# First sweep of an fp32 GLA and conv-FFN layer: row statistics squared in place and summed on VectorE, and one row split at a higher rank

## The chip, the cores and the metric

The kernel runs on one core of a Trainium2 chip. A core has a TensorE (PE; its weight loads are shown apart, as PEld), a VectorE (DVE), a ScalarE (ACT), a GpSimd (POOL) and a SyncE (SP), each working through its own list of instructions in order, and sixteen DMA engines, which take transfers from queues that SP, ACT and POOL issue to. The metric is the device time of one execution in microseconds (us); a run's number is the median of several.

## The reference

One layer over x, 2048 rows of 1024 float32 values. In the first half of the layer the rows are normalized, mixed by a gated linear attention and added back; the second half is a feed-forward network with a causal convolution over the rows:

```python
def rms_normalize(x):
    return x * lax.rsqrt(jnp.mean(x * x, axis=-1, keepdims=True) + EPS)   # EPS = 1e-6
h = rms_normalize(x) * w
proj = h @ w_in                       # columns: q 512, k 512, v 1024, r 1024, gate 16
log_a = log_sigmoid(glr @ w_gate2 + b_gate) / 16
g = cumsum(log_a) in chunks of 64 rows;  k_dec = k * exp(g_end - g)
state = state * exp(g_end) + k_dec^T v;  o = q state        # chunk by chunk, 4 heads
x = x + (rms_normalize(o) * norm_w * silu(r)) @ w_out
...                                   # then the FFN: 1024 -> 5632, convolution, silu(g) * val, 2816 -> 1024
```

## The kernel before

**Products.** Every matrix product of fp32 numbers is made of three products of halves. `split` rounds a block to a short high half on ScalarE (the CAST, L194) and subtracts that from the block on VectorE to get the low half (L195); `mm3p` then multiplies high by low, low by high and high by high (L185, L186, L187). On top of this stands a scheme with seven products in place of eight for a 2 by 2 block of tiles: `PORD` lists them as p1, p5, p6, p2, p7, p3, p4. They need sums and differences of the blocks as operands, which VectorE makes. The 2048 rows are sixteen tiles of 128 rows, and two tiles make a unit, so there are eight units.

**Stages.** The whole is a row of sweeps over the eight units: R (the r columns, and beside them the 16 gate columns), A and B (q, k, v and the scan), Y (w_out), and then the two phases of the FFN. The change touches the first sweep, R. There the rows come in transposed (`xt`, 512 KB a tile) and are multiplied by the norm weight (`hb_t_k`, tile t, half k; L462). The factor 1/rms of a row, `rs[:, t]`, is not in that product: it is put in when a result leaves PE's accumulators, by the evictions on ScalarE (`o_R` L1077 in the first unit, `cp_R` L1220 and `o_R` L1236 later) and on VectorE. So no eviction of tile t can run before `rs` of tile t is known.

**The statistics.** `squares()` makes them from a second load of x, not transposed: `load_rows` (L423, issued by ScalarE) brings half a tile of rows, 128 by 512, into `xr_t_i`, which has two buffers; a Square on ScalarE (L435) sums the squares of each row into `ssq_a`; then ScalarE issues the load of the half after the next one, into the buffer that the Square has just read. The squares themselves are not wanted and go to a tile `junk`, which takes one of the four buffers of the tag "cp"; the evictions `cp_R` use the same four. After a tile's second half GpSimd adds the two sums (L440), scales by 1/1024 and adds EPS (L441) and raises to the power of -0.5 (L442). `squares()` is called nine times by hand in the first unit, and after that four times per unit through a list of delayed calls.

**The first unit.** `first_pair` handles unit 0 with eight plain products m00 to m11 while it makes the operands that unit 1 needs: the weights w_R_p5, w_R_p2, w_R_p6, w_R_p7 (`sum5`, `sum6`, `sum7` in VectorE; each is also split), the differences `ht_1_o` of the rows of unit 1, and the split rows `h_R1_o` (`prep_rows`). The first of these, h_R1_p1, is split from hb_2_0 as it stands.

**The gate.** For each unit the 16 gate columns collect in `pg`, are split into `gstk` (L600 to L602), and for every four tiles a block runs: two matmuls, a softplus, a split into `lh` and `ll`, a cumulative sum on PE (`pd`), its exponential on ScalarE (`e`, L641), four transposes of that on PE (`pe`, L632) and a copy of the totals (`dec`, L634). `e_0_3` below is that exponential for tile 3.

**Order.** A list scheduler of the framework sets each engine's order: among the instructions whose inputs and buffers it expects to be free, it takes the one of the highest priority, which is by default the place in the program; `tc.high_priority(n)` moves it ahead by n. The code's own clock (`later_do`, by modelled PE time) decides at which place a delayed call stands. A tile of a tag with few buffers waits for the last reader of the tile that had the buffer.

Of the kernel before, what the change touches and what calls it, by code (L numbers as in the profile page):

```python
# [12 lines left out]
BF16 = mybir.dt.bfloat16  # L13
AF = mybir.ActivationFunctionType
ALU = mybir.AluOpType

P = 128
EPS = 1e-6
# [7 lines left out]
def hybrid_kernel(  # L26
# [17 lines left out]
    nc = tc.nc  # L44
# [5 lines left out]
    S, D = x.shape  # L50
# [41 lines left out]
    PORD = ("p1", "p5", "p6", "p2", "p7", "p3", "p4")  # L92
# [8 lines left out]
    gp = gx.enter_context(tc.tile_pool(name="gp", bufs=1))  # L101
# [36 lines left out]
    def raw_tile(shape, name):  # L138
        return wr.tile(shape, F32, tag="raw", name=name, bufs=RB)
# [79 lines left out]
    def small(tag, name, n=1):  # L219
        return cst.tile([P, 2], F32, tag=tag, name=name, bufs=4)[:, :n]  # L220
# [198 lines left out]
    def load_rows(m, q):  # L419
        t, i = divmod(m, 2)  # L420
        if t < NTT:
            xrow[m] = rp["h"].tile([P, 512], F32, tag="xr", name=f"xr_{t}_{i}", bufs=2)
            q.dma_start(xrow[m], x[t * P:(t + 1) * P, 512 * i:512 * (i + 1)])  # L423
# [3 lines left out]
    def squares():  # L427

        t, i = divmod(sq["n"], 2)
        r = xrow.pop(sq["n"])  # L430
        if i == 0:
            sq["ssq"] = small("ssq", f"ssq_a{t}", 2)
        ssq = sq["ssq"]
        junk = gp.tile([P, 1024], BF16, tag="cp", name=f"junk_{t}_{i}", bufs=4)
        nc.scalar.activation(junk[:, :512], r, AF.Square, accum_out=ssq[:, i:i + 1])  # L435
        load_rows(sq["n"] + 2, nc.scalar)
        sq["n"] += 1
        if i == 1:
            var = small("var", f"var_a{t}")
            nc.gpsimd.tensor_add(var, ssq[:, 0:1], ssq[:, 1:2])  # L440
            nc.gpsimd.tensor_scalar(var, var, 1.0 / D, EPS, op0=ALU.mult, op1=ALU.add)  # L441
            nc.gpsimd.tensor_tensor(rs[:, t:t + 1], var, neghalf, op=ALU.pow)  # L442

    def hb_tile(name):
# [41 lines left out]
    def prep_row(ps_, j, o):  # L486
        if ps_ == "R":
            need(f"h{j}")
            if o == "p4":
                b21, t2 = hsrc.pop(("p4", j))  # L490
                nc.vector.tensor_sub(b21, b21, t2)
                hsrc[j, o] = b21
            split_row(ps_, j, o, hsrc.pop((j, o)))
        else:
            m = jobs.index((ps_, j, o))
            for n in range(m, min(m + HB - 1, len(jobs))):
                if jobs[n] not in hraw:
                    p_, j_, o_ = jobs[n]
                    hraw[jobs[n]] = row_tile(f"hr_{p_}{j_}_{o_}")
                    nc.sync.dma_start(hraw[jobs[n]], (yd if p_ == "Y" else h1d)[j_, o_])  # L500
            split_row(ps_, j, o, hraw.pop((ps_, j, o)))
# [441 lines left out]
    def prep_rows(n):  # L943
        while done["rows"] < min(n, len(jobs)):
            prep_row(*jobs[done["rows"]])
            done["rows"] += 1
# [25 lines left out]
    def first_pair():  # L972
# [65 lines left out]
        def sum5():  # L1038
            for k in range(2):
                nc.vector.tensor_add(s_[V[k]], a21[V[k]], a22[V[k]])  # L1040
            split_sum("p5", [s_[V[k]] for k in range(2)])
# [49 lines left out]
        for k in range(2):  # L1091
            r = raw_tile([P, 2, 512], f"wr_{ps_}_{k}")
            load_block(put_act, r, ps_, k, (0, 1))
            a12.append(r)
        need_raw[0, 1] = a12
        squares()
        product(1, 0, 0)
        squares()
        product(1, 0, 1)
        squares()  # L1100
        weight("p2", (0, 1), "p2")
        squares()
# [5 lines left out]
        squares()  # L1108
        gate_plain(j, 1, 1, *h[1, 1])
        done["rows"] = len(PORD)  # L1110
        prep_rows(len(PORD) + 1)
        sum5()
        squares()
        product(0, 1, 0)
# [437 lines left out]
    nc.sync.dma_start(nwt, mix_norm_w)  # L1552
    xin[0] = load_xt(0, 2)
    first_pair()
    nc.scalar.dma_start(nw2, ffn_norm_w)
    nc.scalar.dma_start(gw, gla_norm_w)
# [136 lines left out]
```

## Time and profile before

| | |
|---|---|
| runs | 2101.47, 2102.18, 2104.19 us; median 2102.18 |
| the profiled execution | 2099.98 us, of which the traced span 2098.3 us |
| granted clock of TensorE over the span | 0.993 |
| TensorE busy | 98% of the span |
| VectorE, ScalarE, GpSimd busy | 75%, 53%, 33% |

A row of the timeline gives the start and the duration in us, the engine, the line, the operation, what it writes and reads, the shapes, and in brackets how long the engine had waited before it and for what. Names in these rows leave out the numbers of tile and product. Line numbers are those of the kernel before; in the changed one, lines after L441 are one lower up to the second edit.

### The profile page before, as it was taken

The numbers are of one execution on the slowest core, as the hardware profiler recorded it, in microseconds if no ns is written. First come the engines' busy times: TensorE is split into PE (matmuls) and PEld (weight loads), VectorE is DVE, ScalarE is ACT, GpSimd is POOL, SyncE is SP. The second block draws the span as 40 slices with busy tenths as digits, with TensorE's granted clock in tenths as the row PEclk, the third lists the DMA queues.
The fourth block names the chain that finished last, engine by engine and source line by source line (L and its number), as shares of the span: only waits on it lengthen the run. The fifth ranks groups of instructions, "written<-read, shape, count | busy, mean of one in ns | idle before, by whom it ended". The sixth has DMA issues, their size and how long they took to land.

```text
span 2098.3 us, 28206 instructions
## 1 busy us (share of the span) xinstructions
PE 2047.3 (98%) x9700; PEld 1688.9 (80%) x9700; DVE 1583.4 (75%) x2109; ACT 1110.2 (53%) x2022; POOL 683.2 (33%) x595
## 2 busy tenths in 40 slices
PE   6999999999998999999999999999999999999998
PEld 5887788878886887888888887888888888888886
DVE  8766887887888646898898877788888956456564
ACT  5656755675665667645555544455454533223342
POOL 2110000000000003554653553666766433243210
PEclk9999999999999999999999999999999999999999
DMA  9876775577867978545445386545445684554453
GB/s 313 281 236 203 231 235 180 171 248 251 281 199 259 326 259 300 169 138 163 163 138 189 110 281 205 141 111 152 124 130 151 196 326 156 164 167 161 155 214 113
DMA packets 246513, 419.33 MB, mean 200 GB/s; under 512 B 22784, under 2 KB 91520, under 8 KB 246368
## 3 DMA queue, kind: packets, MB, share of 16 engines
q1 hardware_dynamic: 203200, 335.09, 47.4%
q10 hardware_dynamic: 36832, 70.89, 9.9%
q0 software_dynamic: 6336, 11.54, 3.6%
q8 instruction: 76, 1.25, 0.3%
q14 instruction: 69, 0.57, 0.1%
HBM read 278.50 MB, written 150.47 MB: 204 GB/s over the span
## 4 chain that ended last, share of the span: by engine, by line
PE 87%; DVE 4%; DMA 3%; ACT 2%; issue 2%; POOL 1%; SPq 0%; ACTq 0%; DVEq 0%; POOLq 0%
PE ua L186 7%; PE ua L185 7%; PE ua L187 7%; PE pd_p L185 7%; PE pd_p L187 7%; PE pd_p L186 7%; PE uc L185 4%; PE uc L186 4%; PE uc L187 4%; PE mp_A L185 2%; PE mp_Y L185 2%; PE mp_Y L186 2%; PE mp_A L186 2%; PE mp_Y L187 2%; PE mp_A L187 2%; PE mp_B L185 2%
## 5 line engine op out<-in xcount | busy, mean ns | idle before, releaser
L185 PE MATMUL ua<-h_p,uw_p 128*128 128x512 f32 x704 | 274.1, 389 | 2.0 <-ACT c L1306 2.0
L186 PE MATMUL ua<-h_p,uw_p 128*128 128x512 f32 x704 | 274.2, 389 | 1.8 <-DVE uw_p L195 1.8
L187 PE MATMUL ua<-h_p,uw_p 128*128 128x512 f32 x704 | 274.0, 389 | 0.0
L1326 DVE SCALAR_TENSOR_TENSOR t<-u,cw,t 128x1024 f32<-128x1024 f32 x176 | 260.0, 1487 | 6.9 <-ACT t L1323 6.2
L185 PE MATMUL pd_p<-dw_p,da 128*128 128x512 f32 x616 | 239.6, 389 | 0.0
L186 PE MATMUL pd_p<-dw_p,da 128*128 128x512 f32 x616 | 239.6, 389 | 0.0
L187 PE MATMUL pd_p<-dw_p,da 128*128 128x512 f32 x616 | 239.6, 389 | 0.0
L195 DVE TENSOR_TENSOR da<-da_p,da 128x512 fp32r<-128x512 f32 x154 | 119.0, 827 | 82.2 <-ACT da L194 82.2
L195 DVE TENSOR_TENSOR uw_p<-ur,uw_p 128x512 fp32r<-128x512 f32 x176 | 152.8, 885 | 34.9 <-ACT uw_p L194 34.6
L195 DVE TENSOR_TENSOR uw_p<-us,uw_p 128x512 fp32r<-128x512 f32 x132 | 145.3, 1101 | 43.1 <-ACT uw_p L194 43.1
L194 ACT CAST uw_p<-us 128x512 fp32r<-128x512 f32 x132 | 82.1, 622 | 163.9 <-POOL us L1286 105.6
L194 ACT CAST da<-da_p 128x512 fp32r<-128x512 f32 x154 | 84.6, 618 | 144.7 <-PE pd_p L187 104.5
L185 PEld LDWEIGHTS ua<-h_p,uw_p 128*128 128x128 f32 x704 | 132.1, 188 | 30.3 <-ACT c L1306 2.4
L186 PEld LDWEIGHTS ua<-h_p,uw_p 128*128 128x128 f32 x704 | 132.1, 188 | 29.6 <-DVE uw_p L195 2.5
L187 PEld LDWEIGHTS ua<-h_p,uw_p 128*128 128x128 f32 x704 | 132.2, 188 | 27.5
L761 POOL TENSOR_TENSOR rstd<-var,pair 128x2 f32<-128x2 f32 x32 | 22.7, 709 | 403.3 <-DVE var L760 403.3
L1323 ACT ACTIVATE t<-u,cw 128x1024 f32<-128x1024 f32 x88 | 109.6, 1245 | 60.2 <-DVE u L1439 60.0
L185 PE MATMUL uc<-h_p,uw_p 128*128 128x512 f32 x352 | 137.7, 391 | 2.2 <-DMA h_p<-hd_p 2.0
L186 PE MATMUL uc<-h_p,uw_p 128*128 128x512 f32 x352 | 137.4, 390 | 2.0 <-DVE uw_p L195 2.0
L187 PE MATMUL uc<-h_p,uw_p 128*128 128x512 f32 x352 | 137.2, 390 | 0.0
L187 PEld LDWEIGHTS pd_p<-dw_p,da 128*128 128x128 f32 x616 | 115.6, 188 | 24.1
L186 PEld LDWEIGHTS pd_p<-dw_p,da 128*128 128x128 f32 x616 | 115.6, 188 | 24.0
(263 smaller groups left out, 5291.1 us busy)
## 6 DMA issues: line engine op xcount, KB each, us to landing
ur<-in_ffn_w_up_dram SPq DMA_DIRECT2D x84, 512.0 KB, 4.1
da_p<-ad_p SPq DMA_DIRECT2D x154, 256.0 KB, 4.3
ad_p<-t SPq DMA_DIRECT2D x110, 256.0 KB, 2.8
ch<-in_ffn_w_down_dram SPq DMA_DIRECT2D x61, 256.0 KB, 5.0
hr_A_p<-h1d_p SPq DMA_DIRECT2D x56, 256.0 KB, 3.1
hr_B_p<-h1d_p SPq DMA_DIRECT2D x56, 256.0 KB, 3.4
hr_Y_p<-yd_p SPq DMA_DIRECT2D x56, 256.0 KB, 3.8
hd_p<-h2p_p ACTq DMA_DIRECT2D x56, 256.0 KB, 2.0
```

The costliest lines, as they stand in the source:

```text
L185: nc.tensor.matmul(ps_ap, ah, bl, start=(first and i == 0), stop=False, **kw)
L186: nc.tensor.matmul(ps_ap, al, bh, start=False, stop=False, **kw)
L187: nc.tensor.matmul(ps_ap, ah, bh, start=False, stop=(last and i == len(pairs) - 1), **kw)
L194: order["act"] = nc.scalar.copy(hi, src)
L195: nc.vector.tensor_sub(lo, src, f32(hi))
L761: nc.gpsimd.tensor_tensor(rstd, var, neghalf.to_broadcast([P, 2]), op=ALU.pow)
L1323: nc.scalar.activation(t, u[:, 2:2 + TS], AF.Identity, scale=cw[:, 2, c:c + 1], bias=cw[:, 3, c:c + 1])
L1326: nc.vector.scalar_tensor_tensor(t, u[:, k:k + TS], cw[:, k, c:c + 1], t, op0=ALU.mult, op1=ALU.add)
```

## The change

The Square writes onto its own input, `xr`, so the `junk` tile is gone; it scales by 1024 to the power of -0.5 first, so the sums are already means. The sum of both halves and EPS become one VectorE instruction at a raised priority. GpSimd keeps the power alone. In the first unit, the call that splits h_R1_p1 and stores it gets a raised priority.

```diff
--- before.py
+++ after.py
@@ -431,14 +431,13 @@
         if i == 0:
             sq["ssq"] = small("ssq", f"ssq_a{t}", 2)
         ssq = sq["ssq"]
-        junk = gp.tile([P, 1024], BF16, tag="cp", name=f"junk_{t}_{i}", bufs=4)
-        nc.scalar.activation(junk[:, :512], r, AF.Square, accum_out=ssq[:, i:i + 1])
+        nc.scalar.activation(r, r, AF.Square, scale=float(D) ** -0.5, accum_out=ssq[:, i:i + 1])
         load_rows(sq["n"] + 2, nc.scalar)
         sq["n"] += 1
         if i == 1:
             var = small("var", f"var_a{t}")
-            nc.gpsimd.tensor_add(var, ssq[:, 0:1], ssq[:, 1:2])
-            nc.gpsimd.tensor_scalar(var, var, 1.0 / D, EPS, op0=ALU.mult, op1=ALU.add)
+            with tc.high_priority(100):
+                nc.vector.scalar_tensor_tensor(var, ssq[:, 0:1], EPS, ssq[:, 1:2], op0=ALU.add, op1=ALU.add)
             nc.gpsimd.tensor_tensor(rs[:, t:t + 1], var, neghalf, op=ALU.pow)
 
     def hb_tile(name):
@@ -1108,7 +1107,8 @@
         squares()
         gate_plain(j, 1, 1, *h[1, 1])
         done["rows"] = len(PORD)
-        prep_rows(len(PORD) + 1)
+        with tc.high_priority(300):
+            prep_rows(len(PORD) + 1)
         sum5()
         squares()
         product(0, 1, 0)
```

TensorE's list of instructions is the same in both kernels. On the other engines the order changes inside sweep R only. The first place is ScalarE in the first unit, where the weights of unit 1 arrive and tile 0's statistics are made. Before:

```order
L202 DMA wr_R_1_640<-in_gla_w_in_dram 128x2x512
L435 ACTIVATE junk_0_0_643,ssq_a0_642<-xr_0_0_543 128x512
L435 ACTIVATE junk_0_1_660,ssq_a0_642<-xr_0_1_545 128x512
L423 DMA xr_1_0_645<-in_x_dram 128x512
L423 DMA xr_1_1_662<-in_x_dram 128x512
L194 CAST w_R_p2_686<-wr_R_0_638 128x1024
```

and further on, where h_R1_p1 stands:

```order
L1077 ACTIVATE o11_R_0_748<-m11_R_0_668,rs_497 128x512
L435 ACTIVATE junk_2_0_752,ssq_a2_751<-xr_2_0_684 128x512
L600 CAST gstk_536<-pg_0_595 32x256
L423 DMA xr_3_0_754<-in_x_dram 128x512
L602 CAST gstk_536<-pg_0_595 32x256
L194 CAST h_R1_p1_767<-hb_2_0_722 128x512
L194 CAST w_R_p5_773<-ws_p7_511 128x1024
```

After:

```order
L202 DMA wr_R_1_640<-in_gla_w_in_dram 128x2x512
L194 CAST h_R1_p1_760<-hb_2_0_716 128x512
L434 ACTIVATE xr_0_0_543,ssq_a0_642<-xr_0_0_543 128x512
L434 ACTIVATE xr_0_1_545,ssq_a0_642<-xr_0_1_545 128x512
L423 DMA xr_1_0_644<-in_x_dram 128x512
L423 DMA xr_1_1_660<-in_x_dram 128x512
L194 CAST w_R_p2_682<-wr_R_0_638 128x1024
```

The split of h_R1_p1 has moved from behind the second square of unit 1 and both gate casts to a place ahead of the first square.

The second place is VectorE in the same stretch: the low halves (L195), the differences of rows (L449, later L448), and the sums of weights (L1045 and L1052, later L1044 and L1051), of which the second wr_R_0 line opens `sum7`. Before:

```order
L449 TENSOR_TENSOR ht_1_p5_730<-hb_3_0_726,hb_2_0_722 128x512
L195 TENSOR_TENSOR w_R_p5_773<-ws_p7_511,w_R_p5_773 128x1024
L449 TENSOR_TENSOR ht_1_p6_732<-hb_3_1_728,ht_1_p5_730 128x512
L449 TENSOR_TENSOR ht_1_p7_734<-hb_3_1_728,hb_3_0_726 128x512
L1045 TENSOR_TENSOR ws_p7_511<-ws_p7_511 128x1024
L195 TENSOR_TENSOR w_R_p2_686<-wr_R_0_638,w_R_p2_686 128x1024
L195 TENSOR_TENSOR w_R_p2_686<-wr_R_1_640,w_R_p2_686 128x1024
L1052 TENSOR_TENSOR wr_R_0_638<-wr_R_0_638,ws_p7_511 128x1024
L462 TENSOR_TENSOR hb_4_0_964<-xt_4_842,nwt_498 128x512
L462 TENSOR_TENSOR hb_4_1_966<-xt_4_842,nwt_498 128x512
L1057 TENSOR_TENSOR hb_0_0_547<-hb_1_0_551,hb_0_0_547 128x512
L601 TENSOR_TENSOR gstk_536<-pg_0_595,gstk_536 32x256
```

After:

```order
L448 TENSOR_TENSOR ht_1_p5_724<-hb_3_0_720,hb_2_0_716 128x512
L195 TENSOR_TENSOR h_R1_p1_760<-hb_2_0_716,h_R1_p1_760 128x512
L448 TENSOR_TENSOR ht_1_p6_726<-hb_3_1_722,ht_1_p5_724 128x512
L440 SCALAR_TENSOR_TENSOR var_a0_662<-ssq_a0_642 128x1
L448 TENSOR_TENSOR ht_1_p7_728<-hb_3_1_722,hb_3_0_720 128x512
L195 TENSOR_TENSOR w_R_p5_766<-ws_p7_511,w_R_p5_766 128x1024
L1056 TENSOR_TENSOR hb_0_0_547<-hb_1_0_551,hb_0_0_547 128x512
L195 TENSOR_TENSOR w_R_p2_682<-wr_R_0_638,w_R_p2_682 128x1024
L1044 TENSOR_TENSOR ws_p7_511<-ws_p7_511 128x1024
L195 TENSOR_TENSOR w_R_p2_682<-wr_R_1_640,w_R_p2_682 128x1024
L440 SCALAR_TENSOR_TENSOR var_a1_690<-ssq_a1_678 128x1
L1051 TENSOR_TENSOR wr_R_0_638<-wr_R_0_638,ws_p7_511 128x1024
```

The low half of h_R1_p1 now stands second here (it stood behind the gate's L601, after the last row of the first block), the update of hb_0_0 (L1057, then L1056; one of the in-place row differences that `diffs` makes for the later sweeps) has moved up by four, the two new statistics steps (var_a0, var_a1) stand between, and hb_4_0 and hb_4_1 follow behind the last row shown.

The third place is ScalarE about the exponential e_0_3 of the gate. Before:

```order
L194 CAST lh_0_3_1345<-e_0_3_1146 128x512
L641 ACTIVATE e_0_1_1111<-pd_0_1_1269 128x512
L194 CAST h_R3_p5_1335<-ht_3_p5_1254 128x512
L634 COPY dec_494<-pe_1_1307 128x4x2
L641 ACTIVATE e_0_2_1141<-pd_0_2_1316 128x512
L600 CAST gstk_536<-pg_2_1120 32x256
L194 CAST h_R3_p6_1381<-ht_3_p6_1256 128x512
L602 CAST gstk_536<-pg_2_1120 32x256
L634 COPY dec_494<-pe_2_1360 128x4x2
L641 ACTIVATE e_0_3_1146<-pd_0_3_1366 128x512
```

After:

```order
L423 DMA xr_13_0_1903<-in_x_dram 128x512
L640 ACTIVATE e_0_2_1123<-pd_0_2_1294 128x512
L434 ACTIVATE xr_12_1_1824,ssq_a12_1901<-xr_12_1_1824 128x512
L423 DMA xr_13_1_1940<-in_x_dram 128x512
L599 CAST gstk_536<-pg_2_1102 32x256
L194 CAST h_R3_p6_1357<-ht_3_p6_1235 128x512
L434 ACTIVATE xr_13_0_1903,ssq_a13_1993<-xr_13_0_1903 128x512
L601 CAST gstk_536<-pg_2_1102 32x256
L423 DMA xr_14_0_1995<-in_x_dram 128x512
L633 COPY dec_494<-pe_2_1336 128x4x2
L434 ACTIVATE xr_13_1_1940,ssq_a13_1993<-xr_13_1_1940 128x512
L640 ACTIVATE e_0_3_1128<-pd_0_3_1342 128x512
```

Between the square of 5_1 and e_0_3 there were four squares (6_0 to 7_1); now there are sixteen (6_0 to 13_1), each followed by the issue of the load two halves on.

On SyncE the store of h_R1_p1's source, h1d_1_p1, now stands ahead of the stores h1d_0_p2 and h1d_0_p3. GpSimd loses two instructions per tile (32 in all) and VectorE gains one per tile (16).

## The prediction

> **What bounds the kernel now.** I read the page's head first, then TensorE's waits, the windows of the first sweep, the timeline of each engine at the waits that the change touches, and last the tile `xr` with its DMA issues.
>
> ```profile
> span 2098.3 us, 28206 instructions
> PE 2047.3 (98%) x9700; PEld 1688.9 (80%) x9700; DVE 1583.4 (75%) x2109; ACT 1110.2 (53%) x2022; POOL 683.2 (33%) x595
> ```
>
> TensorE is busy for 2047.3 of 2098.3 us, and its instructions stay the same, so the change can only win or lose idle time of TensorE, and the speed at which it restarts. Its waits in the first 300 us (engine, line, tile waited for: total us, times, longest):
>
> ```profile
> PE mp_R L185 <- ACT cp_R L1220: 3.2, 2, 2.2
> PE mp_R L185 <- ACT h_R_p L194: 2.4, 1, 2.4
> PE pe L632 <- ACT e L641: 0.9, 1, 0.9
> PE mp_R L186 <- DVE h_R_p L195: 0.5, 1, 0.5
> ```
>
> These few us are all that the change can remove. What it can add has no such limit: the windows (stretch: length, busy us of PE, PEld, DVE, ACT, POOL with instructions, granted clock, DMA share, GB/s) show a TensorE without a gap from 60 us on, while the DMA engines are loaded to 0.76 and more:
>
> ```profile
> 40.00:50.00 10.00, 8.45 (x34) 6.36 (x34) 9.97 (x13) 8.39 (x16) 4.01 (x5) 0.83 0.98 331
> 50.00:60.00 10.00, 7.81 (x33) 6.11 (x33) 8.52 (x12) 8.76 (x15) 1.92 (x5) 0.83 0.97 338
> 60.00:70.00 10.00, 10.00 (x59) 8.23 (x57) 9.42 (x16) 6.74 (x13) 2.10 (x4) 1.00 0.95 318
> ...
> 80.00:90.00 10.00, 10.00 (x60) 8.17 (x59) 7.32 (x11) 6.75 (x16) 3.38 (x6) 1.00 0.85 259
> 90.00:100.00 10.00, 10.00 (x60) 8.22 (x60) 3.94 (x6) 5.48 (x13) 0.00 (x0) 1.00 0.76 293
> ```
>
> The timeline of TensorE shows both waits and what follows each:
>
> ```profile
> 41.02 0.50 PE L185 MATMUL mp_R<-w_R_p,h_R_p 128*128 128x512 f32 x1 [2.38 <-ACT h_R_p L194]
> 43.38 0.63 PE L187 MATMUL mp_R<-w_R_p,h_R_p 128*128 128x512 f32 x1
> 43.81 0.63 PE L185 MATMUL mp_R<-w_R_p,h_R_p 128*128 128x512 f32 x1
> 47.03 0.39 PE L186 MATMUL mp_R<-w_R_p,h_R_p 128*128 128x512 f32 x1
> 47.26 0.40 PE L187 MATMUL mp_R<-w_R_p,h_R_p 128*128 128x512 f32 x1
> 52.38 0.50 PE L185 MATMUL mp_R<-w_R_p,h_R_p 128*128 128x512 f32 x1 [2.19 <-ACT cp_R L1220]
> ```
>
> Behind a long wait matmuls follow each other every 0.43 us (43.38 to 43.81), later every 0.23 (47.03 to 47.26). The granted clock of 0.83 in both windows says the same: 17% of 10 us lost is some 3.4 us at half speed. So a wait of a few us costs an estimated 1.6 us beside itself (eight matmuls by 0.20).
>
> **The change, part by part: the front.** Splitting h_R1_p1 early takes away the waits of 2.38 and 0.53 us at 41 us. But the end of this stretch is set elsewhere, by VectorE and ScalarE:
>
> ```profile
> 28.19 1.22 DVE L195 TENSOR_TENSOR w_R_p<-ws_p,w_R_p 128x1024 fp32r<-128x1024 f32 x1
> 31.66 2.35 DVE L195 TENSOR_TENSOR w_R_p<-wr_R,w_R_p 128x1024 fp32r<-128x1024 f32 x2
> 33.93 1.22 DVE L1052 TENSOR_TENSOR wr_R<-wr_R,ws_p 128x1024 f32<-128x1024 f32 x1
> 35.07 1.28 DVE L462 TENSOR_TENSOR hb<-xt,nwt 128x512 f32<-128x512 f32 x2
> 36.27 0.68 DVE L1057 TENSOR_TENSOR hb<-hb,hb 128x512 f32<-128x512 f32 x1
> 39.53 0.41 DVE L601 TENSOR_TENSOR gstk<-pg,gstk 32x256 fp32r<-32x256 f32 x1 [2.57 <-ACT gstk L600]
> 41.31 0.68 DVE L195 TENSOR_TENSOR h_R_p<-hb,h_R_p 128x512 fp32r<-128x512 f32 x1
> 41.91 0.68 DVE L1063 TENSOR_TENSOR hb<-hb,hb 128x512 f32<-128x512 f32 x1
> 48.26 1.22 DVE L1052 TENSOR_TENSOR wr_R<-wr_R,ws_p 128x1024 f32<-128x1024 f32 x1
> ...
> 31.65 5.36 POOL L440 TENSOR_TENSOR var_a<-ssq_a 128x1 f32<-128x1 f32 x1 [4.17 <-ACT junk L435]
> 37.37 0.55 POOL L442 TENSOR_TENSOR rs<-var_a,pair 128x1 f32<-128x1 f32 x1
> ...
> 37.96 0.69 ACT L1077 ACTIVATE o_R<-m_R,rs 128x512 f32<-128x512 f32 x1 [5.82 <-POOL rs L442]
> 49.75 1.99 ACT L194 CAST w_R_p<-xsum 128x1024 fp32r<-128x1024 f32 x2 [0.33 <-DVE wr_R L1052]
> 51.65 0.68 ACT L1220 ACTIVATE cp_R<-mp_R,rs 128x512 f32<-128x512 f32 x1
> ```
>
> Read backwards: TensorE's restart at 52.38 waits for the eviction at 51.65, which stands behind the casts at 49.75, which wait for the second L1052 of VectorE at 48.26. VectorE is busy for 9.97 us of the window from 40 to 50, so that row is as late as the row at 39.53 plus the work between. Removing TensorE's wait at 41 gains nothing by itself: TensorE arrives earlier and waits longer for the same eviction. Two things do move the chain.
>
> First, less work in it. The rows at 41.31 and 41.91 follow each other by 0.60 us; both leave the stretch between gstk and the second L1052 (the split goes ahead of it, L1063 behind it): 1.20 us less.
>
> Second, an earlier gstk. It waits for ScalarE, which had stood 5.82 us for rs of tile 1, which GpSimd made in an addition of 5.36 us (beside VectorE rows without a gap) and a power that ended at 37.92. After the change the sum is VectorE's. Its place follows from the order: from 28.19 on stand the split of h_R1_p1 (0.60), two row differences and the hb_0_0 update (0.60 each), four weight rows at 1.14 (the two at 31.66 take 33.93 − 31.66 = 2.27) and a statistics step of 0.07: 7.03 us, so var_a1 ends at about 35.3, and the power, 0.55 us, follows. Ends: it starts at once (35.9, 2.0 earlier), or it is held until VectorE pauses behind hb_4_1, as the addition of 5.36 us was held (38.3, 0.4 later). I take one VectorE row of waiting, 1.14: ready at 37.15, 0.75 earlier.
>
> The Trainium skill, page "SBUF — State Buffer", section "SBUF: two separate sides", describes a port pair shared by VectorE and GpSimd, held exclusively and for a whole instruction by whichever began first; a VectorE step with two SBUF inputs blocks a GpSimd step that reads SBUF. By that rule the power waits for one VectorE row at the most, and the sum would be the one taken here; the addition of 5.36 us over six VectorE rows is longer than the rule gives, and would make it the other end, 1.15 us more.
>
> Front together: −1.20 − 0.75 = −1.95 us (ends −3.2 and −0.8). The half-speed stretch behind 52.38 stays.
>
> **Part by part: steps that I cost at nothing.** VectorE gains sixteen one-column steps; the nearest row is
>
> ```profile
> 10.26 0.15 DVE L518 TENSOR_TENSOR pair<-ident 128x1 f32<-128x1 f32 x1
> ```
>
> where 0.07 us passes to the next row: 1 us over 160 us in which VectorE has 2.7 to 6 us free in ten from 80 us on. If each cost 0.15 in the front, where four stand, it were 0.6 us at most. A Square that writes 128 by 512 float32 in place of bf16 I take to last the same: the eviction at 51.65, of that shape and type, takes 0.68 us against the Square's 0.63, and 0.05 us each is nothing beside the landing of a load. GpSimd loses 32 steps off the path. The store of h1d_1_p1, moved past two stores on SyncE, holds these up until hb_2_0 is there; the blocks that the two copy are not written again before gstk at 39.53, and what they store is read in the next sweep, so nobody waits.
>
> **Part by part: the squares.** This is the step that decides. The junk tile shared four buffers with the evictions `cp_R`, and so the squares were spread out; without it only the two `xr` buffers pace them. A run of loads and squares then stands in ScalarE's list in front of work that TensorE needs: between the square of 5_1 and e_0_3, sixteen squares where there were four. Each must wait until its load has landed, and that load was issued only after the Square two halves before.
>
> ```profile
> 62.70 0.63 ACT L435 ACTIVATE junk<-xr 128x512 bf16<-128x512 f32 x1 [0.85 <-DMA xr<-in_x_dram]
> ...
> L435 ACT ACTIVATE junk<-xr x32: 615/627/633, 23.8 to 183.0; 128x512 bf16<-128x512 f32 x32
> L435 ACT ACTIVATION_READ_ACCUMULATOR junk<-xr x32: 185/188/195, 24.3 to 183.5; 128x1 f32 x32
> ...
> DMA to landing us min/median/max: 2.6/4.8/8.4
> ...
> xr<-in_x_dram ACTq DMA_DIRECT2D x13, 256.0 KB, 4.5
> ...
> 94.06 0.60 ACT L641 ACTIVATE e<-pd 128x512 f32<-128x512 f32 x1 [0.36 <-PE pd L640]
> 96.73 0.44 PE pe L632 x4
> ...
> 181.47 0.66 PE L632 MATMUL pe<-ident,e 128*128 128x128 f32 x4 [0.93 <-ACT e L641]
> ```
>
> The row at 62.70 is the square of 5_1 (it already waits 0.85 for its load); the issue row with x13 is for 60 to 130 us, the row at 94.06 is e_0_3, and at 96.73 stand TensorE's transposes of it. The chain: 5_1 to 13_1 through one buffer is eight links. A link is the Square with its read of the sums (0.53 + 0.19, as the second starts before the first ends: 0.7), 0.1 to issue, and the landing L: 0.8 + L. With the front's gain 5_1 starts at 60.7. L is the unknown: 2.6 at the least, 4.8 the median of all, 4.5 the median of this stretch. I take 4.2: nearest to this stretch's own 4.5, a little less because waiting engines also issue fewer other transfers. Then 13_1 starts at 60.7 + 8 × 5.0 = 100.7 and e_0_3 (0.7 for the square, 0.6 for itself, as at 94.06) is ready at 102.0, where TensorE wants it at 96.73 on the old clock: +5.3 us, the front's gain already used up in it. A wait that long brings a half-speed stretch, +1.6. The wait of 0.93 at 181.47 loses the squares that now run to 183.0 ahead of that exponential: −0.6. Sum: +6.3 us.
>
> On the profiled execution: 2098.3 + 1.7 outside the span = 2099.98, plus 6.3 is 2106.3. The median of the runs shown is 2.2 above it, so I forecast **2108.5**. A change of 0.2%, 4.2 us, is about what a measurement here can tell from none (2098.0 to 2106.4).
>
> How it hangs on L: no wait up to 3.3; the loss eats the gain from 3.4; beyond 0.2% from 3.94 (8 × 4.74 + 60.7 + 1.3 = 99.9, 3.2 late, +1.0); at 4.8, e_0_3 is ready at 106.8, +11.1 in all.
>
> The page "DMA: Bandwidth & Descriptors" of the Trainium skill, section "Anatomy of one DMA — SWDGE (gpsimd) path", gives about 2.0 us fixed and the bytes at 436 GB/s: an estimate of 2.6 us for 256 KB (for GpSimd's queue, where these loads are on ScalarE's). That is this tile's least landing, not its median of 4.8, at a DMA share of 0.76 to 0.95; by the page the squares would never be late, which is the first rival.
>
> **The rivals.** *Loads land quickly* (not slower): ScalarE's queue is lightly used and the loads overlap two by two, so L is below 3.4. For it speaks the least of 2.6; against it the median of 4.5 and twelve more loads of 256 KB in a stretch already at 0.76 to 0.95. Then the front stays, −1.95 − 0.6 = −2.6: 2099.6; between 3.4 and 3.94 it lies within 0.2% too.
>
> *The whole front goes* (faster): the early split lets VectorE run ahead so that both waits and both half-speed stretches vanish: 2.38 + 0.53 + 2.19 + 2 × 1.6 + 0.6 = 8.9, 2093.3. Against it: VectorE's 9.97 of 10 us.
>
> *Loads crowd each other* (more slower): L at 4.8, 2113.3; with the power held as well (+1.2) and a second restart at half speed (+1.6), 2116.1.
>
> **How the numbers follow.** My forecast, squares late with L from 3.94 to about 4.7: 0.36. Crowded loads: 0.20. Quick loads, or a loss that offsets the gain: 0.32. The whole front: 0.12. So slower 0.56, same 0.32, faster 0.12. The range reaches from the quick loads (2099.0, their 2099.6 less half a us) to the crowded (2116.0); it leaves out the faster case and the tail above, under 0.2. My forecast alone spans 2106 to 2113.
>
> **What would show it.** Right: the cast of h_R1_p1 near 26 us and no wait of 2.4 at 41; the restart now at 52.38 near 50.4; the last square by about 115 in place of 183; ScalarE waiting for `xr` loads between 60 and 105, and TensorE for `e` near 95 to 102; busy TensorE still 2047. Wrong: landings of 3 us in that stretch and no wait of TensorE there, an eviction (`cp_R`) or split rows as the late piece in place of `e`, or a power on GpSimd that still lasts several us.

## The result, and the profile after

The changed kernel took 2117.09 us (median of 5 runs, 2113.52 to 2125.43) against 2101.47 us for the kernel before (5 runs, 2097.36 to 2104.19): a ratio of 1.0073, 95% interval 1.0056 to 1.0089. Run a second time, beside other kernels, it was 1.0064 (1.0048 to 1.0079). So the sign was right; the forecast of 2108.5 was too low, and the time lies above the range, which ended at 2116.0.

The head of the page, four of TensorE's waits in the first 300 us, and the windows (columns as before the change):

```profile
span 2116.7 us, 28202 instructions
PE 2050.3 (97%) x9700; PEld 1689.8 (80%) x9700; DVE 1590.1 (75%) x2125; ACT 1109.5 (52%) x2022; POOL 665.4 (31%) x563
```

```profile
PE pe L631 <- ACT e L640: 8.0, 3, 5.0
PE mp_R L185 <- ACT gstk L601: 4.1, 1, 4.1
PE mp_R L185 <- ACT cp_R L1220: 3.0, 2, 2.6
...
PE mp_R L186 <- DVE h_R_p L195: 1.4, 1, 1.4
```

```profile
40.00:50.00 10.00, 7.75 (x34) 5.93 (x33) 9.08 (x13) 7.61 (x16) 0.93 (x1) 0.83 0.92 332
50.00:60.00 10.00, 7.39 (x39) 5.78 (x38) 9.77 (x14) 9.96 (x18) 0.93 (x1) 1.00 0.94 320
60.00:70.00 10.00, 10.00 (x56) 8.22 (x55) 7.61 (x15) 5.80 (x12) 3.71 (x2) 1.00 1.02 350
70.00:80.00 10.00, 5.95 (x25) 4.54 (x24) 5.79 (x11) 5.62 (x14) 1.51 (x2) 0.83 0.82 288
80.00:90.00 10.00, 9.61 (x48) 7.82 (x48) 5.41 (x10) 7.34 (x18) 1.06 (x2) 1.00 0.68 217
90.00:100.00 10.00, 8.55 (x54) 6.83 (x53) 5.31 (x11) 6.56 (x14) 0.97 (x2) 1.00 0.89 307
100.00:110.00 10.00, 4.62 (x22) 3.24 (x20) 2.70 (x6) 4.30 (x13) 1.51 (x2) 1.00 0.75 222
110.00:120.00 10.00, 8.82 (x41) 7.39 (x42) 3.94 (x8) 6.68 (x17) 1.18 (x3) 0.83 0.68 227
```

TensorE was full from 60 to 120 us before; now it is busy for 47.55 of the 60 us from 60 to 120, so 12.45 us idle, and its clock is 0.83 in two of these windows, behind the two longest waits. VectorE and ScalarE are *less* busy there than before: nobody works too long, everybody waits. The timeline shows for whom:

```profile
9.93 0.80 PE L185 MATMUL m_R<-w_R_p,h_R 128*128 128x512 f32 x1 [9.93 <-DVE w_R_p L195]
...
53.66 0.50 PE L185 MATMUL mp_R<-w_R_p,h_R_p 128*128 128x512 f32 x1 [2.61 <-ACT cp_R L1220]
76.59 0.79 PE L185 MATMUL mp_R<-w_R_p,h_R_p 128*128 128x512 f32 x1 [4.05 <-ACT gstk L601]
...
92.18 0.63 PE L631 MATMUL pe<-ident,e 128*128 128x128 f32 x4 [1.45 <-ACT e L640]
102.30 0.66 PE L631 MATMUL pe<-ident,e 128*128 128x128 f32 x4 [1.52 <-ACT e L640]
111.18 1.12 PE L631 MATMUL pe<-ident,e 128*128 128x128 f32 x4 [5.04 <-ACT e L640]
...
227.15 0.39 PE L185 MATMUL mp_A<-w_A_p,h_A_p 128*128 128x512 f32 x1
```

and in the kernel before:

```profile
9.79 0.79 PE L185 MATMUL m_R<-w_R_p,h_R 128*128 128x512 f32 x1 [9.79 <-DVE w_R_p L195]
...
171.74 0.50 PE L185 MATMUL mp_R<-w_R_p,h_R_p 128*128 128x512 f32 x1 [0.98 <-ACT cp_R L1220]
...
213.57 0.39 PE L185 MATMUL mp_A<-w_A_p,h_A_p 128*128 128x512 f32 x1
```

The first and the last row of each fence span sweep R: from the first matmul to the first of sweep A, 203.78 us before and 217.22 after. This length, **sweep R's length** below, leaves out the scatter of the later sweeps: what remains of the span beside sweep R is 1893 to 1901 us in every profile of this document but two (xr3 and xr3_nosplit). It scatters too: a second profile of the changed kernel has 215.3 us. It grew by 13.4 us: 12.45 idle from 60 to 120, 1.1 from the front (53.66 − 9.93 against 52.38 − 9.79), minus 0.98 and 0.93 at 171.74 and 181.47, where the waits are gone; that makes 11.7. The rest, about 1.7, is the clock: each window at 0.83 costs 1.7, and there are three after where there were two.

The cause is in the tile `xr` (first and last start; idle before it; who waited for it), and in the timeline of the engines that serve it:

```profile
L434 ACT ACTIVATE xr<-xr x32: 613/632/637, 26.6 to 118.9; 128x512 f32<-128x512 f32 x32
...
  DMA xr<-in_x_dram: 27.4, 17
...
  DVE var_a L440: 16.3, 8
...
DMA to landing us min/median/max: 2.7/4.6/8.2
```

The squares end at 119 in place of 183, and ScalarE stood 27.4 us for their loads (4.5 in the same view before).

### The profile page after: what moved, and what is told of

It reads as the page before. It is cut to its first block, busy times and chain, and to the rows that moved or that the text cites. A ratio compares the mean times of both kernels' runs of the same rounds, so it can differ in the third digit from the quotient of the medians.

```text
span 2116.7 us, 28202 instructions
## 1 busy us (share of the span) xinstructions
PE 2050.3 (97%) x9700; PEld 1689.8 (80%) x9700; DVE 1590.1 (75%) x2125; ACT 1109.5 (52%) x2022; POOL 665.4 (31%) x563
## 3 DMA queue, kind: packets, MB, share of 16 engines
q8 instruction: 76, 1.25, 0.2%
## 4 chain that ended last, share of the span: by engine, by line
PE 66%; DVE 10%; POOL 7%; DMA 7%; issue 7%; ACT 3%; SPq 0%; POOLq 0%; DVEq 0%; ACTq 0%
PE pd_p L186 6%; PE pd_p L187 6%; PE pd_p L185 6%; PE ua L186 4%; PE ua L187 4%; PE ua L185 4%; DMA xr<-in_x_dram 3%; DVE uw_p L195 3%; PE mp_A L185 2%; DVE t L1326 2%; POOL as_p L1356 2%; PE mp_B L185 2%; PE mp_Y L185 2%; PE mp_Y L186 2%; PE mp_A L186 2%
## 5 line engine op out<-in xcount | busy, mean ns | idle before, releaser
L195 DVE TENSOR_TENSOR da<-da_p,da 128x512 fp32r<-128x512 f32 x154 | 121.0, 839 | 82.7 <-ACT da L194 75.8
L195 DVE TENSOR_TENSOR uw_p<-ur,uw_p 128x512 fp32r<-128x512 f32 x176 | 153.2, 888 | 35.5 <-ACT uw_p L194 35.2
L195 DVE TENSOR_TENSOR uw_p<-us,uw_p 128x512 fp32r<-128x512 f32 x132 | 145.9, 1105 | 40.3 <-ACT uw_p L194 40.3
L187 PEld LDWEIGHTS ua<-h_p,uw_p 128*128 128x128 f32 x704 | 132.1, 188 | 27.4
L1323 ACT ACTIVATE t<-u,cw 128x1024 f32<-128x1024 f32 x88 | 109.6, 1245 | 59.7 <-DVE u L1439 59.5
```

Source lines behind the costliest of these rows:

```text
L187: nc.tensor.matmul(ps_ap, ah, bh, start=False, stop=(last and i == len(pairs) - 1), **kw)
L195: nc.vector.tensor_sub(lo, src, f32(hi))
L1323: nc.scalar.activation(t, u[:, 2:2 + TS], AF.Identity, scale=cw[:, 2, c:c + 1], bias=cw[:, 3, c:c + 1])
```

## Experiments

Lengths of sweep R are read as above, from one profiled execution of each kernel, and among the kernels whose squares no cp buffer holds back differences of 2 to 4 us say nothing (the changed kernel and after_again are one kernel, and so are inplace_split and gpsimd_sums); ratios are to the kernel before, on the same chip.

| kernel | sweep R, us | ratio | 95% interval |
|---|---|---|---|
| before | 203.8 | 1 | |
| changed | 217.2 | 1.0073 | 1.0056 to 1.0089 |
| junk_back | 204.2 | 1.0004 | 0.9995 to 1.0013 |
| inplace_only | 212.4 | 1.0053 | 1.0040 to 1.0066 |
| split_only | 205.0 | 1.0004 | 0.9994 to 1.0013 |
| vec_only | 204.9 | 1.0007 | 0.9997 to 1.0016 |
| own_junk | 221.0 | 1.0069 | 1.0056 to 1.0083 |
| no_split | 216.3 | 1.0052 | 1.0040 to 1.0064 |
| inplace_split | 214.5 | 1.0056 | 1.0043 to 1.0069 |
| no_loads | 202.9 | 0.9991 | 0.9981 to 1.0001 |
| xr3 | 208.3 | 1.0161 | 1.0143 to 1.0179 |
| xr3_nosplit | 210.6 | 1.0162 | 1.0145 to 1.0178 |
| no_pow | 201.6 | 0.9991 | 0.9981 to 1.0002 |
| no_pow_split | 202.4 | 0.9992 | 0.9980 to 1.0005 |
| xr3b | 208.1 | 1.0040 | 1.0027 to 1.0053 |
| after_again | 215.3 | 1.0064 | 1.0048 to 1.0079 |
| gpsimd_sums | 218.7 | 1.0070 | 1.0057 to 1.0083 |

**Which part costs.** junk_back is the changed kernel with one edit taken back:

```diff
-        nc.scalar.activation(r, r, AF.Square, scale=float(D) ** -0.5, accum_out=ssq[:, i:i + 1])
+        junk = gp.tile([P, 1024], BF16, tag="cp", name=f"junk_{t}_{i}", bufs=4)
+        nc.scalar.activation(junk[:, :512], r, AF.Square, scale=float(D) ** -0.5, accum_out=ssq[:, i:i + 1])
```

> The changed kernel with the squares written to the junk tile of the tag cp again; the scaling, the VectorE sum and the early split stay. Theory (pacing: without the cp buffer the squares are hoisted into ScalarE's list and its in-order waits for loads reach TensorE): nearly the whole loss goes; what is left is the front, whose restart came 1.3 us later (53.66 against 52.38), so 0 to +3 us against before, no wait of TensorE for gstk or e between 70 and 115 us. Rival (the VectorE sums and the early split cause the loss, the front's delay growing through the sweep): at least half stays, +8 us or more.

inplace_only makes that edit alone, without the scaling, in the kernel before:

```diff
-        nc.scalar.activation(junk[:, :512], r, AF.Square, accum_out=ssq[:, i:i + 1])
+        nc.scalar.activation(r, r, AF.Square, accum_out=ssq[:, i:i + 1])
```

> The kernel before with the squares written in place, and nothing else of the change. Theory (pacing): +10 to +14 us, with the waits of TensorE for gstk and e of the changed kernel, a little earlier since the front is not late. Rival (sums and split cause it): below +4 us.

The window of junk_back, 60 to 120 us, has a full TensorE again:

```profile
60.00:120.00 60.00, 60.00 (x333) 49.31 (x333) 40.85 (x68) 35.56 (x73) 4.89 (x6) 1.00 0.82 275
```

With the junk tile back the whole loss is gone (2101.58 against 2101.79 us), and the last square starts at 184.0 us again; in place alone loses 10.8 us (2112.55). The loss is that of the first edit.

**The write or the buffer.** own_junk writes to a junk tile again, but not to one of the evictions' buffers:

```diff
-        nc.scalar.activation(r, r, AF.Square, scale=float(D) ** -0.5, accum_out=ssq[:, i:i + 1])
+        junk = rp["h"].tile([P, 512], BF16, tag="junk", name=f"junk_{t}_{i}", bufs=1)
+        nc.scalar.activation(junk, r, AF.Square, scale=float(D) ** -0.5, accum_out=ssq[:, i:i + 1])
```

> The changed kernel, but the squares go to a bf16 junk tile again, one with a tag of its own (one buffer, 1 KB), not to the four cp buffers that the evictions use. Theory (what matters is that the squares no longer wait for a cp buffer): the same loss as the changed kernel, +11 to +17 us, with waits of TensorE for gstk and e between 70 and 115 us. Rival (writing float32 onto its own input is what costs, by holding the tile or by a slower Square): as with junk in the cp buffers, -1 to +2 us.

Its waits of TensorE from 60 to 120 us:

```profile
PE pe L632 <- ACT e L641: 7.4, 3, 4.1
PE mp_R L185 <- ACT gstk L602: 2.9, 1, 2.9
```

The same two waits (beside 2.3 us once for an eviction of VectorE), and a loss in the same band (+14.6 us). A Square takes 0.632 us in the median when it writes onto its input and 0.627 in the kernel before, so the write costs nothing that shows; what costs is that the square no longer waits for a cp buffer.

**The squares or their loads.** no_loads keeps the early squares and takes their loads away:

```diff
         t, i = divmod(m, 2)
-        if t < NTT:
+        if 2 <= m < 2 * NTT:
+            xrow[m] = keep2[m % 2]
+        elif t < NTT:
```

> The changed kernel without the loads of rows from tile 1 on: each Square goes over one of the first two xr tiles again (so the statistics of tiles 1 to 15 are not those of x). All 32 squares still stand early in ScalarE's list, even earlier, ahead of e_0_3. Theory (the price is ScalarE's wait for the landings, not the squares' own time): the waits of TensorE for gstk and e go, 0 to +3 us. Rival (thirty squares of 0.7 us ahead of the evictions and the gate are themselves the delay): some 28 x 0.7 = 20 us of ScalarE work in 60 to 105 us, TensorE waits 5 us or more, +6 us or more.

Its squares, first and last start:

```profile
L438 ACT ACTIVATE xr<-xr x32: 614/624/639, 26.8 to 76.4; 128x512 f32<-128x512 f32 x32
```

and its TensorE waits from 60 to 120 us:

```profile
PE mp_R L185 <- ACT cp_R L1224: 3.8, 1, 3.8
PE mp_R L185 <- DVE o_R L1166: 0.9, 1, 0.9
PE mp_R L185 <- ACT gstk L605: 0.3, 1, 0.3
```

The wait for gstk is down to 0.3 us, those for e are gone, and the time is that of before (2099.81 against 2101.60 us), although all 32 squares have run by 77 us. They still delay an eviction once by 3.8 us, so the squares' own time isn't free; but the loss is the waiting for landings. This kernel also takes thirty loads of 256 KB off the DMA engines, which by itself could help other transfers; that ScalarE's own waits for `xr` are the cause is read from the 27.4 us above and from the rows of the chain below.

**The number of links.** With a third xr buffer fewer landings lie one behind the other. xr3 (and xr3_nosplit, the same without the early split) took the room from the cp tag; xr3b uses the fourth cp buffer for xr in sweep R alone:

```diff
-            xrow[m] = rp["h"].tile([P, 512], F32, tag="xr", name=f"xr_{t}_{i}", bufs=2)
+            xrow[m] = rp["h"].tile([P, 512], F32, tag="xr", name=f"xr_{t}_{i}", bufs=3)
...
-        load_rows(sq["n"] + 2, nc.scalar)
+        if sq["n"] == 0:
+            load_rows(2, nc.scalar)
+        load_rows(sq["n"] + 3, nc.scalar)
...
-        return gp.tile([P, 512], F32, tag="cp", name=name, bufs=4)
+        return gp.tile([P, 512], F32, tag="cp", name=name, bufs=3)
```

> The changed kernel with three xr buffers in place of two, each load issued one half earlier; the room comes from the cp tag, three buffers in place of four now that no junk uses it. Theory (each link of the chain is a landing that ScalarE waits out in order; with three buffers two of three landings lie beside other work): from the square of 5_1 to that of 14_0, now the last ahead of e_0_3, there are 17 halves over 3 buffers, 5.7 links by 5.6 us = 32 us in place of 44.5, so e_0_3 is at most 1 us late: 0 to +4 us against before. Rival (the landings are bound by what the DMA engines move, so a third load in flight only makes each landing half as long again): +9 us or more, landings of 6 us and more.

> The same without the early split. Theory: as the last, 1 us less: -1 to +3 us. Rival: +6 us or more.

Both missed by far, with +35.0 and +34.8 us. In this sweep the loss did fall, from 13.4 to 4.5 and 6.8 us, but less than the theory said: in xr3 the squares from 5_1 to 14_0 took 39.2 us (64.19 to 103.37), not 32, and TensorE began the transposes of e_0_3 6.6 us later than before, counted from its first matmul, where e_0_3 was to be at most 1 late. The median landing from 60 to 120 us was 4.4 us, so the rival's 6 did not come either. The rest of the loss lies in later sweeps. The waits of TensorE in the FFN of xr3, and below them those of the kernel before:

```profile
PE ua L185 <- ACT c L1308: 13.4, 11, 8.2
```

```profile
PE ua L185 <- ACT c L1306: 2.0, 1, 2.0
```

So there too the evictions seem to need the fourth cp buffer. xr3b leaves it to them:

```diff
+            if m % 3 == 2:
+                xrow[m] = gp.tile([P, 512], F32, tag="cq", name=f"xr_{t}_{i}", bufs=1)
+            else:
...
+        if "_R_" not in name:
+            cps["n"] += 1
+            if cps["n"] % 4 == 0:
+                return gp.tile([P, 512], F32, tag="cq", name=name, bufs=1)
+        return gp.tile([P, 512], F32, tag="cp", name=name, bufs=3)
```

> The changed kernel with a third xr buffer that is the fourth cp buffer during sweep R alone; the later sweeps and the FFN use all four in turn as before. Theory (number of links times landing): sweep A starts 5 to 7 us later than in the kernel before, as with three buffers and a smaller cp tag (+5.8), and the time is 4 to 8 us above before, about half the loss of the changed kernel. Rival (the loss hangs on what the DMA engines move or on the squares' place alone): +12 us or more.

Its sweep R is 4.4 us longer than before, a third of the changed kernel's loss (by the clock sweep A begins 5.65 us later, as expected, but 1.3 of these are a later first matmul), and the time 9.2 us above before: more than the 4 to 8 expected, below the rival's 12. ScalarE's waits for `xr` loads fell from 27.4 to 8.3 us. So a third buffer takes most of the waiting away; the chain itself, 40.7 us from 5_1 to 14_0 (44.5 to 13_1 in the changed kernel), shrank far less than by the number of its links, and these runs don't show what holds it. That the whole time stays above what the sweep lost is within the scatter of the later sweeps, or a cost of the odd buffer there; these runs don't separate the two.

**The other two edits beside the squares in place.** no_split and inplace_split each take one more edit out of the changed kernel (the raised priority of `prep_rows`; the VectorE sum).

> The changed kernel without the early split: squares in place, sum on VectorE. In place alone cost +10.8 us, the whole change +15.6. If the early split makes up the difference (it holds ScalarE 2 us for hb_2_0 and so puts off the loads and the whole chain of squares): +9 to +12 us. If the VectorE sum does (it puts the small steps into VectorE's row where ScalarE's late squares hold them up): +14 to +17 us.

> The kernel before with squares in place and the early split, sums on GpSimd as before. The other half of the same question: +14 to +17 us if the early split makes up the difference of 4.8 us, +9 to +12 us if the VectorE sum does.

Both came out at the lower figure (+10.8 and +10.4 us), which neither theory allows for both. So the changed kernel ran once more beside inplace_split on one chip, there named gpsimd_sums:

> The changed kernel itself, beside the next on one chip. Both theories: +14 to +17 us, as measured before.

> The changed kernel with the sums on GpSimd again (squares in place, early split). If the VectorE sums cost something of their own, by making VectorE wait for late squares (16.3 us in eight waits): 4 to 6 us less than the changed kernel on the same chip. Rival (the earlier difference was one of chips and rounds): within 2 us of it.

Now the changed kernel lost 13.1 us (14 to 17 expected) and the one without the VectorE sum 16.2, 3 us more, where 4 to 6 less or the same within 2 was expected. The same kernel gave +10.4 on one chip and +16.2 on another; the five kernels with unpaced squares and two xr buffers all lie in that band, and no order among them can be told. The 5 us that I had put down to the VectorE sums can't be told from scatter.

**The front.** split_only and vec_only are the kernel before with one of the other edits.

> The kernel before with the early split of h_R1_p1 alone. Theory: ScalarE now waits about 2 us for hb_2_0 ahead of the first square, so the loads of tile 1's rows are issued some 4 us later, rs of tile 1 is later, and the restart of p6 comes 1.5 to 3 us after 52.38; +1 to +3 us in all. Rival (as I forecast: the split leaves VectorE's stretch behind gstk and gains 0.6 to 1.2 us): -1 us.

> The kernel before with the scaling and the sum of both halves in one VectorE step; junk and the split as before. Theory: the power on GpSimd is still held by VectorE's rows (4.87 us in the changed kernel for the first), so rs of tile 1 comes 0 to 1.5 us earlier and the whole moves by 0 to -1.5 us, not measurable. Rival (GpSimd's additions were the cause of the late gstk): the restart comes 2 us or more earlier and the time falls by 2 to 4 us.

Neither moves the time. The restart of p6, counted from the first matmul (42.59 before), is 43.03 and 42.65: no gain of the −1.95 I forecast, and not the full loss expected of split_only either. But the second profile of the changed kernel, after_again, has its restart at 41.48 where the first has 43.73, so one profile each can't tell such differences from none. no_pow asks what an early rs would be worth, no_pow_split adds the split at a priority of 30:

```diff
-            var = small("var", f"var_a{t}")
...
-                nc.vector.scalar_tensor_tensor(var, ssq[:, 0:1], EPS, ssq[:, 1:2], op0=ALU.add, op1=ALU.add)
-            nc.gpsimd.tensor_tensor(rs[:, t:t + 1], var, neghalf, op=ALU.pow)
+                nc.vector.scalar_tensor_tensor(rs[:, t:t + 1], ssq[:, 0:1], EPS, ssq[:, 1:2], op0=ALU.add, op1=ALU.add)
```

> The kernel before with the sums on VectorE and no power: the VectorE step writes rs itself (so rs is the mean square plus EPS, not its power of -0.5), and GpSimd has nothing in this sweep. It asks whether the front would have gained had rs of tile 1 come early. Theory (the front's chain was read rightly, only the power stayed blocked beside VectorE, 7.9 us for two of 0.55): rs of tile 1 comes 4 us earlier, gstk up to 2.5 us earlier, the restart of p6 (43.2 before, counted from TensorE's first matmul: 52.38 - 9.79 = 42.6) 1 to 2.5 us earlier, and the time falls by 1 to 3 us. Rival (something else holds the front, such as the landing of the rows of tile 2): restart within 0.5 us of 42.6, no change of time.

> The last with the split of h_R1_p1 raised by 30, which puts it behind the squares of tile 1 and ahead of that of 2_0. Theory: the split has left the stretch behind gstk too, 0.6 us more: the restart 2 to 3 us earlier than 42.6, the time 2 to 4 us lower. Rival: as no_pow within 0.5 us.

(The 43.2 there is a slip; the value is the 42.6 behind it.) ScalarE's timeline in no_pow:

```profile
35.36 0.69 ACT L1075 ACTIVATE o_R<-m_R,rs 128x512 f32<-128x512 f32 x1 [1.63 <-DVE rs L440]
...
38.62 0.63 ACT L435 ACTIVATE junk<-xr 128x512 bf16<-128x512 f32 x1 [2.57 <-DMA xr<-in_x_dram]
...
39.25 0.34 ACT L598 CAST gstk<-pg 32x256 fp32r<-32x256 f32 x1
```

rs of tile 1 is there at 35.3 and the eviction that waited for it starts at 35.36 (37.96 before). But the next row is the square of 2_0, and its load lands only at 38.6; gstk follows at 39.25, where it was at 39.15. From the first matmul that is 1.0 us earlier, and the restart 1.3 (41.27), in no_pow_split 0.5 us (42.13, where 2 to 3 were expected). Neither these nor the times, −1.5 and −1.7 us, can be told from none. What the rows do show is that behind the one wait stood another, nearly as late.

## Why the prediction was too low

**The squares: the mechanism was right.** The last square at 119 (forecast: by 115), ScalarE's waits for `xr` from 60 us on, TensorE's for e (at 92, 102 and 111; forecast near 95 to 102), busy TensorE unchanged within 3 us: all near what the prediction said it would show. What failed is the size of the chain of squares. The rows of the chain from 5_1 to e_0_3, with two of the front and three in the middle:

```profile
26.10 0.62 ACT L194 CAST h_R_p<-hb 128x512 fp32r<-128x512 f32 x1 [2.09 <-DVE hb L461]
...
37.00 0.63 ACT L434 ACTIVATE xr<-xr 128x512 f32<-128x512 f32 x1 [2.15 <-DMA xr<-in_x_dram]
...
65.41 0.63 ACT L434 ACTIVATE xr<-xr 128x512 f32<-128x512 f32 x1 [1.61 <-DMA xr<-in_x_dram]
...
75.43 0.63 ACT L434 ACTIVATE xr<-xr 128x512 f32<-128x512 f32 x1 [2.57 <-DMA xr<-in_x_dram]
...
76.18 0.36 ACT L601 CAST gstk<-pg 32x256 fp32r<-32x256 f32 x1
...
77.66 0.63 ACT L434 ACTIVATE xr<-xr 128x512 f32<-128x512 f32 x1
...
79.53 0.63 ACT L434 ACTIVATE xr<-xr 128x512 f32<-128x512 f32 x1 [1.15 <-DMA xr<-in_x_dram]
79.54 0.34 ACTq L423 DMA_DIRECT2D xr<-in_x_dram  x1
...
109.92 0.63 ACT L434 ACTIVATE xr<-xr 128x512 f32<-128x512 f32 x1 [0.56 <-DMA xr<-in_x_dram]
...
110.55 0.58 ACT L640 ACTIVATE e<-pd 128x512 f32<-128x512 f32 x1
```

e_0_3 was ready at 111.1, forecast 102.0. Of the 9.1 us:

- *The start of the chain* (forecast 60.7, measured 65.41): 4.7.
- *The landing L* (forecast 4.2): the eight landings of the chain were 4.66, 5.79, 3.42, 3.10, 3.11, 5.35, 2.67 and 6.55 us, mean 4.3: 1.0. So this term, which I held for the unknown, was right, and the rival of crowded loads (4.8) wrong in it, though its time was nearer; the second restart at half speed, which that rival added, did come.
- *The rest of a link* (forecast 0.8): 44.51 us for eight links is 5.56 each, minus 4.3 leaves 1.25: 3.5. Each link passes through ScalarE's list. At 79.54 the load of 8_1, whose buffer had been read from 77.66 to 78.4, is issued only when square 8_0 has got its own data after 1.15 us. And the load of 10_1, issued at 87.82, had landed at 90.9, but its square ran at 92.96, behind an exponential of the gate and two casts. These two places are 3.1 of the 3.5. The links of both buffers and the work between them are one chain, not two.

The second profile of the changed kernel (after_again) has the same links, 44.45 us for eight, with a mean landing of 4.3; its chain starts 53.4 us after the first matmul, where the first profile has 55.5 and the forecast 50.9 (60.7 − 9.79).

**From e_0_3 to the time.** Counted from its first matmul, TensorE began the transposes of e_0_3 14.3 us later than before (111.18 − 9.93 against 96.73 − 9.79); forecast was 5.3. From there to sweep A it took 0.9 us less than before: the two waits of 0.98 and 0.93 are gone, where I had counted −0.6, and a stretch at half speed is added, as forecast (+1.6); some 0.6 us of it I can't place. 14.3 − 0.9 is the 13.4 us of the sweep, against the 6.3 of my sum. So the lateness of e_0_3 is the term that was too small.

I summed one wait of TensorE, at e_0_3. There are five from 60 us on; the second longest, 4.05 at 76.59, is for gstk of unit 1 (76.18 above, behind a square that waits 2.57), to which I gave no price. These waits don't add to the sum: all five lie ahead of the transposes of e_0_3, inside the 14.3 us. But they show that late squares hold up every piece of work behind them in ScalarE's list. An eviction or split rows as the late piece in place of `e` was my sign of being wrong; gstk, the split of the gate columns, was a late piece beside `e`.

**The front: no gain came.** I moved the start of the chain ahead by a gain of 1.95 us, and placed var_a1 at 35.3 by adding up VectorE's rows, as if only VectorE's order moved. (That sum has a slip: 35.3 + 1.14 + 0.55 is 36.99, not 37.15.) On ScalarE the raised split (before, it stood behind 2_0, the first square of unit 1) stands ahead of the first squares and waits 2.09 us there for hb_2_0, with the squares and their loads queued behind it. The load of 1_1 went out at 29.0 (25.2 before), its square ran at 37.00, and VectorE, in its own order, stood for it:

```profile
34.88 1.23 DVE L195 TENSOR_TENSOR w_R_p<-wr_R,w_R_p 128x1024 fp32r<-128x1024 f32 x1 [0.60 <-ACT w_R_p L194]
37.75 0.16 DVE L440 SCALAR_TENSOR_TENSOR var_a<-ssq_a 128x1 f32<-128x1 f32 x1 [1.64 <-ACT xr L434]
...
29.82 4.87 POOL L441 TENSOR_TENSOR rs<-var_a,pair 128x1 f32<-128x1 f32 x1 [27.36 <-DVE var_a L440]
37.99 1.47 POOL L441 TENSOR_TENSOR rs<-var_a,pair 128x1 f32<-128x1 f32 x1 [3.30 <-DVE var_a L440]
```

So in this profile the restart came 1.1 us later in place of 1.95 earlier. In after_again the same split waits the same 2.09 us, but the load of 1_1 lands in 4.7 us, not 8.0, and VectorE doesn't stand for it; there the power is what is held:

```profile
35.76 0.15 DVE L440 SCALAR_TENSOR_TENSOR var_a<-ssq_a 128x1 f32<-128x1 f32 x1
...
30.25 8.41 POOL L441 TENSOR_TENSOR rs<-var_a,pair 128x1 f32<-128x1 f32 x2 [27.79 <-DVE var_a L440]
```

var_a1 is then done 25.5 us after the first matmul, as forecast, and rs of tile 1 still 0.2 us later than before; the restart comes 1.1 us earlier. So the earlier gstk that I forecast (0.75) came in neither profile, the other part of the gain (1.20) can't be told from the scatter, and how much of the late start of the chain is the early split's doing stays open: the start lies 53.1 and 53.4 us after the first matmul in the two kernels with early squares and two buffers that lack the split (inplace_only, no_split), and 53.4 to 59.5 in the five such profiles with it (two of the changed kernel, inplace_split, gpsimd_sums, own_junk).

The Trainium skill's page "SBUF — State Buffer" (section "SBUF: two separate sides") says that of a GpSimd step that reads SBUF and a VectorE step with two SBUF inputs, whichever begins first holds the shared ports for its whole instruction. I read that as a wait of one VectorE row at the most. This fits the power of 1.47, close to the 1.69 I had taken, and does not fit the 4.87, which ended only when VectorE paused at 34.3 to 34.88, five rows on, nor the two in 8.41. A power that lasts several us was one of my signs of being wrong. The Trainium skill's page "DMA: Bandwidth & Descriptors" (section "Anatomy of one DMA — SWDGE (gpsimd) path") gave an estimate of 2.6 us a load (for GpSimd's queue); the least landing of this run is 2.7, the mean in the chain 4.3, and the measurement decides.

## What to carry to other kernels

A scratch tile that shares buffers with something on the critical path is also a throttle: before it is removed, ask what it holds back, and where an in-order engine would stand if that ran ahead. Look for instructions that wait for a transfer in a list ahead of work that the bottleneck needs; here one more transfer in flight took away some two thirds of the sweep's loss. When a wait is moved on one engine, follow each engine that it touches: in one profile a cast put ahead of squares delayed loads, the loads a sum, and the sum the stretch that the cast was to shorten. And take a second profile of the same kernel before a difference of 1 to 2 us in one stretch is given a cause.

## What was not expected of the hardware

A GpSimd step of one column, 0.55 us by itself, took 4.87 us beside VectorE rows without a pause; in vec_only two of them took 7.88:

```profile
30.21 7.88 POOL L442 TENSOR_TENSOR rs<-var_a,pair 128x1 f32<-128x1 f32 x2 [27.74 <-DVE var_a L441]
```

Their ends lie behind small gaps in VectorE's work: in vec_only the first power ended at 35.09, just behind VectorE's one-column step at 34.58, and the second at 38.1, just after it paused at 37.7. But the power of 1.47 us in the changed kernel ended behind a single row of 1.22, and why some are let through so and others not, these runs don't tell. And three cp buffers in place of four cost xr3 some 30 us outside sweep R (35.0 − 4.5), where the waits for the FFN's evictions grew from 2.0 to 13.4 us; where the rest of the 30 went wasn't followed.
